# Ring weight slots 64 bytes longer, split weights placed 0 or 64 bytes into them by their role, operand pairs in one tile

## The chip, the cores and the metric

The kernel runs on one core of one Trainium2 chip. The metric is the device time of one execution in microseconds (us); smaller is better. Several executions are taken of a kernel, and their median is compared.

## The reference, cut to what matters

Two transformer layers work on 512 latent and 256 context tokens of 1024 features, all in float32. Layer 0 mixes the tokens by grouped attention (16 query heads, 4 key heads), layer 1 by a gated linear recurrence in two directions (HGRN2). Each is followed by a feed-forward block, and shifts, scales and gates are computed from a condition vector.

```python
for i in range(DEPTH):
    mod_l = (silu(c) @ ada_w[i] + ada_b[i])          # 6 shifts, scales and gates, likewise for ctx
    hn_l = modulate(rms_norm(h, norm_mix_w[i]), sh1_l, sc1_l)
    y_l, y_c = attention_mixer(...) if i % 2 == 0 else hgrn2_mixer(...)
    h = h + gt1_l * y_l
    h = h + gt2_l * swiglu(modulate(rms_norm(h, norm_ffn_w[i]), sh2_l, sc2_l), ffn_w_in[i], ffn_w_out[i])
    ...                                              # hc likewise in layer 0
return rms_norm(h, final_norm_w)
```

## The kernel before, in words

**Three products for one.** TensorE takes its operands as pairs: a float32 tile is split into a rounded high part and the rest (`split`, line 88: ScalarE casts the high part at line 90, VectorE or GpSimd subtracts at line 95). `mm3` (lines 116 to 120) then issues three matmuls into one accumulator: line 118 multiplies high by high, line 119 the high held part by the low streamed part, line 120 the low held part by the high streamed part. The operand that is loaded into the array with LDWEIGHTS, 128x128, is called held here, and the one that passes through it, 128 partitions by 256, 384 or 512 elements, streamed. The profile writes `out<-streamed,held`.

**Where operands lie.** Weights arrive by DMA in a ring of buffers: four slots `raw`, three `whi` and three `wlo`, each of 1024 floats per partition (4096 bytes), handed out in turn by the pool `ring` (`load_split`, line 99; `ring_tile`, line 1010). Normalized activations lie in pools of their own: `hnh`/`hnl` (attention input), `xb11`, `xb21`, `xb12`, `xb22`, `xw`, `xt1` to `xt4` (feed-forward operands, each with a high and a low tile), `gh`/`gl` (hidden units). Some pools begin with a tile named `shift` of 16 or 24 floats that nothing reads; it moves the pool's other tiles by 64 or 96 bytes.

**The stages, in order of time.** Attention: `kv` and `q` (activations held, weights streamed), `sc` (scores), softmax with its scaling on GpSimd (line 779), transposes `pt<-ident,pf` (line 789), `po`, then the projections `wo` and `wos`. Feed-forward 0, by a two-level scheme of seven products on half-size blocks (`x`, `y`, `z`, `w`; weights held, activations streamed at a width of 384) after some plain columns `ffi`; its output `ffo` has widths 256 and 512. HGRN: projections `hv`, `hg` (activations held, weights streamed, width 256), `hq`, `hz` (weights held, activations streamed, widths 512 and 256), the scan `lv` (line 1730), `hwo`. Feed-forward 1: as before, `ffi`, `x`, `y`, `z`, `w` at a width of 256, and `ffo` at 512 from `foh`/`fol`, whose slots are reused every second unit (`split_next`, line 1290).

**What sets the order.** A scheduler orders each engine's instructions by readiness and by when slots come free; two tiles that are parts of one allocation share their release. `residual` (line 760) adds a finished `ffo` to the stream `hT` on VectorE. `modc` holds the modulation columns (one tile per layer); four small fills of it are on GpSimd (line 263).

Of the kernel before, what the change touches and what calls it, by code (L numbers as in the profile page):

```python
# [16 lines left out]
P = 128  # L17
D = 1024
# [26 lines left out]
TAIL_BUDGET = (8, 1.6)  # L45
LEVELS = [1, 2, 4, 8, 16, 32, 64]
# [3 lines left out]
def kernel(  # L50
# [48 lines left out]
    def load_split(src, shape, name, eng=None, hi_eng=None):  # L99
        n = 1  # L100
        for s in shape[1:]:
            n *= s

        def get(kind, dt, bufs):
            t = ring.tile([P, 1024], dt, tag=kind, bufs=bufs, name=f"{kind}_{name}")
# [65 lines left out]
    csil = cst.tile([P, 2, KT], F32, name="csil")  # L171

# [30 lines left out]
    def ada_chunk(ch, pa, rows, load):  # L203
# [8 lines left out]
        ada_put(pa, rows(), modc[0][:, ch : ch + 1], ada_bias(0, ch, 1), 1, KT, pt)  # L212

    def ada_acc(layer, ch, nv, fp, wide):
# [38 lines left out]
        def folded():  # L253
            pc = bank(f"adc{layer}{ch}")
            mv = part[:, 0:nv].rearrange("p v (k j) -> p j k v", j=4)
            for j in range(4):
                PE.matmul(pc[32 * j : 32 * (j + 1), 0 : KT * nv], fold, mv[:, j], start=True, stop=True)
            DVE.tensor_tensor(
                modc[layer][:, ch, :, 0:nv], pc[:, 0 : KT * nv].rearrange("p (k v) -> p k v", v=nv),
                cols1[:, 32 + layer * 48 + ch * 8 :][:, 0:KT].unsqueeze(2).to_broadcast([P, KT, nv]), op=ALU.add,  # L260
            )
            if nv == 1:
                POOL.memset(modc[layer][:, ch, :, 1], 0.0)
# [45 lines left out]
    def modulate(es_pool, hs, rst, which, layer, hn_hi, hn_lo, spans):  # L309
        a_c = cst.tile([P, KT, 2], F32, name=f"a_{which}{layer}")  # L310
# [3 lines left out]
            a_c, modc[layer][:, csc], 1.0, nwv.unsqueeze(2).to_broadcast([P, KT, 2]),  # L314
# [27 lines left out]
    hn_hi, hn_lo = hn_tiles(hnp)  # L342
    qst = pool("qkvst", qes, side="right")
# [57 lines left out]
    a_c0 = cst.tile([P, KT, 2], F32, name="a_c0")  # L401
# [5 lines left out]
    def ada_group(gi, k0, n):  # L407
# [3 lines left out]
        for kk in range(0, KT, per):  # L411
# [28 lines left out]
    def ada_shared(ch, nsum):  # L440
# [113 lines left out]
    qT = [qt_tile(g) for g in range(KVH)]  # L554
    kTt = keep.tile([P, 2 * KVH, T], F32R, name="kT")
# [208 lines left out]
    ap_.tile([P, 16], F32, name="shift")  # L764
# [41 lines left out]
    def wo_gen(g, oh, ol):  # L806
        wo = [load_split(attn_w_o[0, k * P : (k + 1) * P, :], [P, D], f"wo{k}", POOL) for k in (2 * g, 2 * g + 1)]
# [27 lines left out]
    def third(h, t):  # L835
# [5 lines left out]
        if h % 2 == 1 and t == NT - 1:  # L841
# [30 lines left out]
    acc_n = pool("accn").tile([P, T], F32, name="acc_n")  # L872
# [76 lines left out]
    def ffn(layer, only_lat, pre, begin, tail=None):  # L949
# [7 lines left out]
        if layer:  # L957
            fp.tile([P, 16], F32, name="shift")

        def operand(m, slot=None):  # L960
# [6 lines left out]
            return [p_.tile([P, 4, H], F32R, tag=f"x{slot or m}{c}", name=f"x{m}{c}") for c in "hl"]  # L967
# [42 lines left out]
        def ring_tile():  # L1010
            return [ring.tile([P, 1024], F32R, tag=t, bufs=3, name=f"{t}_w") for t in ("whi", "wlo")]
# [975 lines left out]
```

## Time and profile before

| | us |
|---|---|
| median of three executions | 1793.43 |
| lowest and highest of them | 1792.02, 1795.57 |
| the profiled execution's own time | 1796.98 |
| its span, first to last instruction | 1795.1 |
| TensorE matmul busy | 1738.7 (97%) |
| TensorE weight loads busy, beside the matmuls | 1594.5 (89%) |
| VectorE busy | 1304.2 (73%) |
| ScalarE busy | 871.7 (49%) |
| GpSimd busy | 623.6 (35%) |

The profiled execution lies 3.55 us above the median, and 1.88 us of it lie outside the span. A matmul's listed duration reaches from its start to its modelled end and overlaps the next matmul; what a row of matmuls costs is the distance from start to start, which the timeline of TensorE shows.

### The profile page before, as it was taken

How to read it: one execution, taken by the hardware profiler on the slowest of the kernel's cores; microseconds unless marked ns; L12 is line 12 of the kernel's file. 1: busy time of each engine (PE TensorE's matmuls, PEld its weight loads, DVE VectorE, ACT ScalarE, POOL GpSimd, SP SyncE). 2: the span in 40 equal slices, each digit the busy share in tenths (PEclk: the TensorE clock that was granted, in tenths of full speed). 3: DMA queues.
4: the chain of work that ended last, by engine and by line, in shares of the span. 5: the costliest groups of instructions: out<-in, count | busy, mean ns of one | idle time of the engine just before them, and what ended most of it. 6: DMA issues, size and time to landing. Idle time of an engine off the chain costs nothing.

```text
span 1795.1 us, 30616 instructions
## 1 busy us (share of the span) xinstructions
PE 1738.7 (97%) x11717; PEld 1594.5 (89%) x11717; DVE 1304.2 (73%) x2281; ACT 871.7 (49%) x1777; POOL 623.6 (35%) x570
## 2 busy tenths in 40 slices
PE   8999999999999999999999999999999899999998
PEld 5788788988899989999998989898898898999996
DVE  4876688888888878887866565665747659886764
ACT  3454777776632524343345444343434445554545
POOL 1354355444112404131313343234425454433420
PEclk9999999999999999999999999999999899999999
DMA  8543410002034243445331122122211123333322
GB/s 310 192 130 119 152 36 25 24 1 77 24 106 124 69 131 94 150 133 159 100 118 46 60 71 64 54 83 84 77 53 46 58 60 115 101 111 105 100 61 84
DMA packets 213457, 166.42 MB, mean 93 GB/s; under 512 B 7952, under 2 KB 190400, under 8 KB 213312
## 3 DMA queue, kind: packets, MB, share of 16 engines
q1 hardware_dynamic: 213024, 163.43, 29.7%
q8 instruction: 92, 1.51, 0.3%
q10 hardware_dynamic: 288, 1.05, 0.1%
q14 instruction: 53, 0.43, 0.1%
HBM read 162.36 MB, written 2.10 MB: 92 GB/s over the span
## 4 chain that ended last, share of the span: by engine, by line
PE 78%; DVE 8%; ACT 5%; issue 3%; POOL 3%; DMA 1%; SPq 0%; POOLq 0%; DVEq 0%; ACTq 0%
PE ffo L118 5%; PE ffo L120 5%; PE ffo L119 5%; PE x L120 3%; PE x L119 3%; PE x L118 3%; PE lv L1730 3%; PE pt L789 3%; PE y L118 2%; PE y L119 2%; PE y L120 2%; PE hz L119 2%; PE hz L118 2%; PE hz L120 2%; PE sc L729 1%
## 5 line engine op out<-in xcount | busy, mean ns | idle before, releaser
L1737 POOL TENSOR_TENSOR KD<-KD,tot 128x384 f32<-128x384 f32 x96 | 102.5, 1091 | 79.9 <-ACT kc L1720 76.1
L779 POOL TENSOR_SCALAR pf<-pf,st 128x768 f32<-128x768 f32 (+1 forms) x96 | 73.6, 769 | 125.5 <-DVE st L778 89.3
L761 DVE SCALAR_TENSOR_TENSOR hT<-ffo,modc,hT 128x512 f32<-128x512 f32 (+1 forms) x122 | 78.4, 648 | 43.5 <-PE ffo L120 43.4
L120 PE MATMUL ffo<-gh,wlo_w 128*128 128x512 f32 (+1 forms) x304 | 102.4, 337 | 0.0
L119 PE MATMUL ffo<-gl,whi_w 128*128 128x512 f32 (+1 forms) x304 | 102.1, 336 | 0.0
L118 PE MATMUL ffo<-gh,whi_w 128*128 128x512 f32 (+1 forms) x304 | 101.8, 338 | 0.0
L242 DVE SCALAR_TENSOR_TENSOR adacc<-adw,csil,adacc 128x512 f32<-128x512 f32 x98 | 83.2, 859 | 8.7 <-DMA adw<-in_ada_w_dram 8.6
L95 DVE TENSOR_TENSOR ptl<-pt,pth 128x384 fp32r<-128x384 f32 (+1 forms) x160 | 79.8, 523 | 12.5 <-ACT pth L90 11.3
L90 ACT CAST pth<-pt 128x384 fp32r<-128x384 f32 (+1 forms) x160 | 69.9, 461 | 33.9 <-PE pt L789 22.1
L777 ACT ACTIVATE pf<-sc,st 128x768 f32<-128x768 f32 (+1 forms) x96 | 73.5, 765 | 18.9 <-DVE st L775 18.0
L1737 DVE TENSOR_TENSOR QD<-QD,tot 128x256 f32<-128x256 f32 x96 | 52.5, 587 | 40.6 <-PE lv L1730 40.4
L775 DVE TENSOR_REDUCE st<-sc 128x1 f32<-128x768 f32 (+1 forms) x96 | 74.0, 772 | 10.1 <-PE sc L730 8.7
L1720 ACT COPY kc<-KD 128x256 f32<-128x256 f32 x112 | 43.3, 413 | 75.2 <-PE lv L1730 44.8
L789 PE MATMUL pt<-ident,pf 128*128 128x128 f32 x448 | 72.2, 275 | 5.1 <-DVE ptl L95 3.8
L118 PE MATMUL ffo<-gh,foh 128*128 128x512 f32 (+1 forms) x186 | 71.3, 383 | 0.0
L120 PE MATMUL ffo<-gh,fol 128*128 128x512 f32 (+1 forms) x186 | 70.6, 380 | 0.2 <-DVE fol L95 0.2
L119 PE MATMUL ffo<-gl,foh 128*128 128x512 f32 (+1 forms) x186 | 70.7, 380 | 0.0
L1730 PE MATMUL lv<-QD,kc 128*128 128x128 f32 x448 | 63.8, 287 | 4.5 <-DVE QD L1737 2.3
L1796 POOL TENSOR_SCALAR oss<-oss 128x4 f32<-128x4 f32 (+1 forms) x9 | 4.7, 524 | 180.2 <-DVE oss L1795 180.1
L1730 PEld LDWEIGHTS lv<-QD,kc 128*128 128x128 f32 x448 | 59.1, 192 | 8.5 <-issue 4.3
L789 PEld LDWEIGHTS pt<-ident,pf 128*128 128x128 f32 x448 | 51.4, 140 | 13.8 <-issue 6.2
L120 PEld LDWEIGHTS ffo<-gh,wlo_w 128*128 128x128 f32 x304 | 57.3, 188 | 6.6
(1114 smaller groups left out, 6762.3 us busy)
## 6 DMA issues: line engine op xcount, KB each, us to landing
adw<-in_ada_w_dram SPq DMA_DIRECT2D x40, 512.0 KB, 4.6
adw<-in_ada_w_dram SPq DMA_DIRECT2D x80, 256.0 KB, 2.9
raw_hz<-in_hgrn_w_in_dram SPq DMA_DIRECT2D x14, 512.0 KB, 3.8
adr<-in_ada_w_dram SPq DMA_DIRECT2D x16, 256.0 KB, 5.9
adr<-in_ada_w_dram SPq DMA_DIRECT2D x8, 512.0 KB, 7.3
raw_wq<-in_attn_w_qkv_dram SPq DMA_DIRECT2D x8, 512.0 KB, 4.8
raw_wo<-in_attn_w_o_dram SPq DMA_DIRECT2D x8, 512.0 KB, 3.5
raw_hv<-in_hgrn_w_in_dram SPq DMA_DIRECT2D x8, 512.0 KB, 5.1
```

Of the source, the lines that this page charges most:

```text
L95: m = (eng or DVE).tensor_tensor(lo, src, hi.bitcast(F32), op=ALU.subtract)
L118: PE.matmul(ps, ahi, bhi, start=first, stop=False, **kw)
L119: PE.matmul(ps, ahi, blo, start=False, stop=False, **kw)
L120: PE.matmul(ps, alo, bhi, start=False, stop=last, **kw)
L242: pin(DVE.scalar_tensor_tensor(a, raw, cc, a, op0=ALU.mult, op1=ALU.add))
L761: DVE.scalar_tensor_tensor(hT[o][:, a:e], ps, mcol(layer, ch, o, v), hT[o][:, a:e], op0=ALU.mult, op1=ALU.add)
L775: DVE.tensor_reduce(st3[:, 0:1], ps[:, :nk], op=ALU.max, axis=AX.X, negate=True)
L777: ACT.activation(pf, ps[:, :nk], AF.Exp, bias=st3[:, 0:1], accum_out=st3[:, 1:2])
L779: POOL.tensor_scalar(pf, pf, st3[:, 2:3], 1.0, op0=ALU.mult, op1=ALU.mult)
L789: PE.transpose(pt[:, i * P : (i + 1) * P], pf[:, (i0 + i) * P : (i0 + i + 1) * P], ident)
L1730: PE.matmul(ps[:, cs], kc[:, cs], mv, start=True, stop=True)
L1737: eng.tensor_tensor(view, view, f, op=ALU.mult)
```

## The change

Per partition, a ring slot of `whi` and `wlo` gets 1040 floats in place of 1024. `ring_pair` hands out 1024 of them, beginning at float 0 or 16 of the slot; a table of which of the three slots lies where (`RING_BASE`) decides between the two so that a weight that is streamed begins at 0 modulo 128 bytes, and one that is held (`still=1`) at 64. High and low parts of a feed-forward operand, of a normalized HGRN operand and of an `fo` weight share one tile, again with an offset by role. The modulation columns of both layers share one tile `modc` of seven columns (layer 1's sixth uses the seventh), the scale tiles are renamed to one name `a_c`, and pads `shift`, `shift0` to `shift3` are added where others go.

```diff
+SHIFT = 16
+RING_BASE = {"whi": (1, 1, 0), "wlo": (0, 0, 1)}
...
+    def ring_pair(name, still):
+        got = []
+        for tag, bases in RING_BASE.items():
+            off = SHIFT if bases[pairs[0] % 3] != still else 0
+            t = ring.tile([P, 1024 + SHIFT], F32R, tag=tag, bufs=3, name=f"{tag}_{name}")
+            got.append(t[:, off : off + 1024])
+        pairs[0] += 1
+        return got
...
-        raw, hi, lo = get("raw", F32, 4), get("whi", F32R, 3), get("wlo", F32R, 3)
+        raw = view(ring.tile([P, 1024], F32, tag="raw", bufs=4, name=f"raw_{name}"))
+        hi, lo = map(view, ring_pair(name, still))
...
-    modc = [cst.tile([P, 6, KT, 2], F32, name=f"modc{l}") for l in range(2)]
+    modc = cst.tile([P, 7, KT, 2], F32, name="modc")
+
+    def mods_of(layer, chunk):
+        return modc[:, 6 if layer and chunk == 5 else chunk]
...
-                POOL.memset(modc[layer][:, ch, :, 1], 0.0)
+                POOL.memset(mods_of(layer, ch)[:, :, 1], 0.0)
...
-    ap_.tile([P, 16], F32, name="shift")
...
-        wo = [load_split(attn_w_o[0, k * P : (k + 1) * P, :], [P, D], f"wo{k}", POOL) for k in (2 * g, 2 * g + 1)]
+        wo = [load_split(attn_w_o[0, k * P : (k + 1) * P, :], [P, D], f"wo{k}", POOL, still=int(g == 0))
+              for k in (2 * g, 2 * g + 1)]
...
-        if layer:
-            fp.tile([P, 16], F32, name="shift")
+        def xpair(p_, tag, name, still):
+            if p_ is hnp:
+                return hn_pair(tag, name, still)
+            t = p_.tile([P, 8 * H + 32], F32R, tag=f"x{tag}", name=f"x{name}")
+            at = 16 * still
+            return [t[:, at : at + 4 * H], t[:, at + 4 * H : at + 8 * H]]
...
         def ring_tile():
-            return [ring.tile([P, 1024], F32R, tag=t, bufs=3, name=f"{t}_w") for t in ("whi", "wlo")]
+            return ring_pair("w", 1)
...
-                    tiles[ti] = [fp.tile([P, 640], F32R, tag=f"fo{c}", bufs=2, name=f"fo{c}") for c in "hl"]
+                    t = fp.tile([P, 1280 + 32], F32R, tag="fo", bufs=2, name="fo")
+                    tiles[ti] = [t[:, 16:656], t[:, 656:1296]]
                 elif ti not in tiles:
-                    tiles[ti] = [fp.tile([P, 3 * 512], F32R, tag=f"x{ti}{c}", name=f"fo{ti}{c}") for c in "hl"]
+                    tiles[ti] = xpair(fp, ti, f"fo{ti}", 1)
...
-    hnp.tile([P, 16], F32, name="shift")
+    hn_base = {"b11": 0, "b21": 1, "t4": 0, "b22": 1}
+
+    def hn_pair(tag, name, still):
+        t = hnp.tile([P, 8 * 384 + SHIFT], F32R, tag=f"x{tag}", name=f"x{name}")
+        at = SHIFT if hn_base[tag] != still else 0
+        return [t[:, at : at + 1536], t[:, at + 1536 : at + 3072]]
```

What the edits do to addresses can be read from the tile addresses of the two built programs. The table gives, for each group of matmuls, the first byte of the streamed and of the held operand modulo 128, before and after, and how many matmuls it holds. The last two rows are float32 matmuls, counted as the profile does, twice for each non-transpose.

| group (width) | matmuls | before: streamed, held | after |
|---|---|---|---|
| q (256) | 576 | 0, 96 | 0, 64 |
| hv, hg (256) | 960 | 0, 64 | 0, 64 |
| hz (256 and 512), hq (512) | 840 | 64, 0 | 64, 0 |
| x, y, z, w of feed-forward 1 (256) | 1512 | 64, 0 | 0, 64 |
| x, y, z, w of feed-forward 0 (384) | 1680 | 64, 0 | 0, 64 |
| ffo from ring weights (256; 512) | 456; 456 | 64, 0 | 0, 64 |
| ffo from foh, fol, fot (256; 512) | 132; 570 | 64, 64 | 0, 64 |
| ffi from ring weights (256) | 240 | 64, 0 | 0, 64 |
| ffi from w01, w11 (256) | 144 | 64, 64 | 0, 64 |
| hwo, wo (256; 512) | 240; 288 | 0, 0 | 0, 64 or 64, 0 |
| wos (384) | 96 | 0, 0 | 0, 64 |
| ffi of feed-forward 0 (384), a quarter each | 48; 48 | 64, 64 | 0, 64; 0, 0 |
| kv (512) | 144 | 0, 96 | 0, 64 |
| po (256) | 448 | 64, 0 | 0, 64 |
| sc (256; 512) | 192; 128 | 0, 0 | 0, 64 |
| transposes pt (128) | 448 | 0, 64 | 0, 0 |
| scan lv of line 1730 (128) | 448 | 96, 96 | 32, 32 |

The order of instructions on TensorE, ScalarE and SyncE's queue stays. Two engines have rows that move. On VectorE, near the end of feed-forward 1 (`residual` is line 761 before and 779 after; the split of an output weight is line 95 before and 97 after), before:

```order
2063 L761 SCALAR_TENSOR_TENSOR hT_1979<-ffo,modc_83,hT_1979 128x512
2064 L95 TENSOR_TENSOR fol<-raw_('fo', 4, 2)_18754,foh 128x640
2065 L95 TENSOR_TENSOR fol<-raw_('fo', 4, 3)_18760,foh 128x640
2066 L761 SCALAR_TENSOR_TENSOR hT_1980<-ffo,modc_83,hT_1980 128x512
2067 L279 TENSOR_TENSOR acc_n<-acc_n,sq_18944 128x512
```

and after:

```order
2063 L779 SCALAR_TENSOR_TENSOR hT_1981<-ffo,modc,hT_1981 128x512
2064 L779 SCALAR_TENSOR_TENSOR hT_1982<-ffo,modc,hT_1982 128x512
2065 L97 TENSOR_TENSOR fo<-raw_('fo', 4, 2)_18696,fo 128x640
2066 L97 TENSOR_TENSOR fo<-raw_('fo', 4, 3)_18701,fo 128x640
2067 L296 TENSOR_TENSOR acc_n<-acc_n,sq_18879 128x512
```

The second residual now stands ahead of the two splits. The same swap of one split and one residual occurs at the splits `('fo', 0, 2)` and `('fo', 0, 4)` at the start of feed-forward 1. On GpSimd the four fills of `modc` stand together at the program's start before:

```order
13 L165 TENSOR_TENSOR fold<-ident 128x32
14 L436 MEMSET pick 128x64
15 L263 MEMSET modc_83 128x8 x4
16 L167 TENSOR_TENSOR fold<-fold,ident 128x32
17 L438 MEMSET pick 128x1 x2
```

After, one stays there, one stands among the softmax scalings, and two at the start of feed-forward 0, of which this is the first (line 97 is the split's subtraction, 296 the sum of squares, 280 the fill):

```order
186 L296 TENSOR_TENSOR acc_n<-acc_n,sq_5473 128x384
187 L280 MEMSET modc 128x8
188 L97 TENSOR_TENSOR xb_5270<-x_5493,xb_5270 128x384
189 L311 TENSOR_TENSOR rc<-rc,mhalf 128x3
```

Three fills have moved to later rows. No other row has moved there, and no row was added or dropped on any engine.

Because the high and the low part of `fo` are now one tile, the ScalarE cast of a new high part waits for the last matmul that reads the slot's low part (line 120) and no longer for the one before it that reads the high part (line 119).

More of the change, by code (lines that the diff above doesn't have):

```diff
@@ L102, in load_split, with view @@
             n *= s
-        def get(kind, dt, bufs):
-            t = ring.tile([P, 1024], dt, tag=kind, bufs=bufs, name=f"{kind}_{name}")
+        def view(t):
             t = t[:, :n]
@@ L211, in ada_chunk @@
             yield
-        ada_put(pa, rows(), modc[0][:, ch : ch + 1], ada_bias(0, ch, 1), 1, KT, pt)
+        ada_put(pa, rows(), modc[:, ch : ch + 1], ada_bias(0, ch, 1), 1, KT, pt)
     def ada_acc(layer, ch, nv, fp, wide):
@@ L400 @@
     DVE.tensor_copy(cols1, pr[:, 0:P])
-    a_c0 = cst.tile([P, KT, 2], F32, name="a_c0")
+    a_c = cst.tile([P, KT, 2], F32, name="a_c")
     adv = ada_w[0].rearrange("(k p) (ch n) -> p k ch n", p=P, ch=6)
@@ L554 @@
     qT = [qt_tile(g) for g in range(KVH)]
+    keep.tile([P, SHIFT], F32, name="shift1")
     kTt = keep.tile([P, 2 * KVH, T], F32R, name="kT")
@@ L966, in operand @@
                 return [wide_op[0][:, i], wide_op[0][:, i + 1]]
-            return [p_.tile([P, 4, H], F32R, tag=f"x{slot or m}{c}", name=f"x{m}{c}") for c in "hl"]
+            if not layer and m == "t2":
+                return [p_.tile([P, 4, H], F32R, tag=f"x{m}{c}", name=f"x{m}{c}") for c in "hl"]
+            return [v_.rearrange("p (k n) -> p k n", k=4) for v_ in xpair(p_, slot or m, m, 0)]
         wide_op = []
         xops = {m: operand(m, slot) for m, slot in (("b11", None), ("b21", None), ("b12", "t4"), ("b22", None))}
-        a_c = cst.tile([P, KT, 2], F32, name=f"a_ffn{layer}")
         DVE.scalar_tensor_tensor(
-            a_c, modc[layer][:, 4], 1.0, cols1[:, 16 + layer * KT :][:, 0:KT].unsqueeze(2).to_broadcast([P, KT, 2]),
+            a_c, mods_of(layer, 4), 1.0, cols1[:, 16 + layer * KT :][:, 0:KT].unsqueeze(2).to_broadcast([P, KT, 2]),
             op0=ALU.add, op1=ALU.mult,
@@ L983, in gslot @@
         def gslot(i, dt, name):
-            p_ = late_pool[0] if not layer and i in (0, 1, 8, 9) else fp
-            return p_.tile([P, n], dt, tag=f"g{i}", name=name)
+            late = not layer and i in (0, 1, 8, 9)
+            t = (late_pool[0] if late else fp).tile([P, n], dt, tag=f"g{i}", name=name)
+            if late and i not in late_pool:
+                late_pool.append(i)
+                if len(late_pool) == 5:
+                    late_pool[0].tile([P, SHIFT], F32, name="shift3")
+            return t
         raws, loads, groups = {}, [], {}
@@ L1024, in plain_split @@
                 slot, p_ = {(0, 1): (3, fp), (1, 0): (1, fp), (1, 1): (2, fp if layer else hnp)}[j, i]
-                t = [p_.tile([P, 4 * H], F32R, tag=f"xt{slot}{c}", name=f"w{j}1{c}")[:, 0:1024] for c in "hl"]
+                if p_ is hnp:
+                    t = [p_.tile([P, 4 * H], F32R, tag=f"xt{slot}{c}", name=f"w{j}1{c}")[:, 0:1024] for c in "hl"]
+                else:
+                    t = [v_[:, 0:1024] for v_ in xpair(p_, f"t{slot}", f"w{j}1", 1)]
             pool_ = (j, i) == (0, 0) or j > 1 and i if layer else j == 0
@@ L1820, in wo_pair @@
     def wo_pair(pr_):
-        wo = [load_split(hgrn_w_o[0, k * P : (k + 1) * P, :], [P, D], f"hwo{k}") for k in (2 * pr_, 2 * pr_ + 1)]
+        wo = [load_split(hgrn_w_o[0, k * P : (k + 1) * P, :], [P, D], f"hwo{k}", still=1) for k in (2 * pr_, 2 * pr_ + 1)]
         if pr_ == GH // 2 - 2:
@@ L1838, in hgrn_wo_last @@
         for k in ks:
-            t = [ring.tile([P, 1024], F32R, tag=tag, bufs=3, name=f"{tag}_hwo{k}") for tag in ("whi", "wlo")]
+            t = ring_pair(f"hwo{k}", 1)
             split(t[0], t[1], hv.pop(("w", k)))
```

30 lines of the change are left out of this document (17 added, 13 removed).

## The prediction

> **What bounds the kernel now.** The page comes first: engines, the clock in 40 slices, and the chain that ended last.
>
> ```profile
> span 1795.1 us, 30616 instructions
> PE 1738.7 (97%) x11717; PEld 1594.5 (89%) x11717; DVE 1304.2 (73%) x2281; ACT 871.7 (49%) x1777; POOL 623.6 (35%) x570
> PEclk9999999999999999999999999999999899999999
> PE 78%; DVE 8%; ACT 5%; issue 3%; POOL 3%; DMA 1%; SPq 0%; POOLq 0%; DVEq 0%; ACTq 0%
> ```
>
> TensorE is busy 97% of the span, at a clock granted in full nearly throughout, and 78% of the chain is its own. So the time is the number of matmuls times the distance from one to the next. The change leaves the number and the order on TensorE alone. It can only pay through that distance, and the distance must then depend on addresses, for it alters nothing else there.
>
> The timeline of TensorE shows that the distance differs within one width. Here is the plain `ffi` stage of feed-forward 1 at width 256. Weights of `w11` (held at 64, streamed at 64) come first, then ring weights (held at 0) under the same line numbers.
>
> ```profile
> 1458.08 0.28 PE L118 MATMUL ffi<-xb22h,w11h 128*128 128x256 f32 x1
> ...
> 1458.44 0.28 PE L118 MATMUL ffi<-xw,whi_w 128*128 128x256 f32 x1
> ...
> 1459.46 0.28 PE L118 MATMUL ffi<-xw,whi_w 128*128 128x256 f32 x1
> ```
>
> Three matmuls take 0.36 us where both operands share their residue modulo 128, so 120 ns each; the nine after them take 1.02 us, 113.3 ns each. Next the first and last rows of four other runs at width 256: `hv` (15 steps, streamed 0, held 64), `x` and `z` of feed-forward 1 (19 steps, 64, 0), `q` (14 steps, 0, 96), `hwo` (15 steps, 0, 0).
>
> ```profile
> 998.82 0.28 PE L120 MATMUL hv<-whi_hv,hnb21l 128*128 128x256 f32 x1
> ...
> 1000.52 0.28 PE L120 MATMUL hv<-whi_hv,hnb22l 128*128 128x256 f32 x1
> ```
>
> ```profile
> 1599.73 0.28 PE L118 MATMUL x<-xw,whi_w 128*128 128x256 f32 x1
> ...
> 1601.96 0.28 PE L119 MATMUL z<-xw,whi_w 128*128 128x256 f32 x1
> ```
>
> ```profile
> 149.76 0.28 PE L118 MATMUL q<-whi_wq,hnh 128*128 128x256 f32 x1
> ...
> 151.40 0.28 PE L120 MATMUL q<-whi_wq,hnl 128*128 128x256 f32 x1
> ```
>
> ```profile
> 1419.78 0.28 PE L120 MATMUL hwo<-oth,wlo_hwo 128*128 128x256 f32 x1
> ...
> 1421.56 0.28 PE L120 MATMUL hwo<-oth,wlo_hwo 128*128 128x256 f32 x1
> ```
>
> That is 1.70/15 = 113.3 ns for `hv`, 2.23/19 = 117.4 for `x`, 1.64/14 = 117.1 for `q` and 1.78/15 = 118.7 for `hwo`. `hv` and `q` are the same code shape with other addresses. There are thus three paces: 113.3 (fast), about 117.3 (slow), 119 to 120 (same residue). The `ffi` run and `x` show that the first two are not told apart by addresses alone: both are 64 against 0.
>
> **The change, part by part.**
>
> *Width 256.* All these groups go to 0 against 64, as `hv` and `hg` have it, except `hz`, one pair of `wo` tiles and some small groups. How often such a group keeps the fast pace I read from means over whole groups, by the view that groups by line and shape:
>
> ```profile
> L119 PE MATMUL hv<-wlo_hv,hnb21h 128*128 128x256 f32 x48 | 13.3, 277 | 0.0
> L120 PE MATMUL x<-xw,wlo_w 128*128 128x256 f32 x72 | 20.1, 280 | 0.0
> L120 PE MATMUL ffi<-xb12h,wlo_w 128*128 128x256 f32 x20 | 5.5, 276 | 0.0
> ```
>
> The durations keep the distances' differences: 276 for a run that is all fast, 280 all slow, and `hv` at 277. It holds the fast pace for about three quarters of its matmuls. I take this share for every group that gets `hv`'s addresses. The sum, each count from the table of groups and the price as slow distance minus 113.3: `x`, `y`, `z`, `w` of feed-forward 1, 1512 x 4.1 ns = 6.2 us; `q`, 576 x 3.8 = 2.2; `ffo` of feed-forward 0, whose rows follow, 456 x (1.65 us/14 - 113.3 = 4.6) = 2.1; `hwo` and `wo`, 240 x 5.4 = 1.3; the 276 with equal residues, 276 x 6.7 = 1.8. Together 13.6, of which three quarters are **10.2 us** gained. `po` and `sc` wait too often in their rows for a price; they are taken at nothing, with 448 x 3.3 = 1.5 more as the other bound.
>
> ```profile
> 546.32 0.28 PE L118 MATMUL ffo<-gh,whi_w 128*128 128x256 f32 x1
> ...
> 547.97 0.28 PE L120 MATMUL ffo<-gh,wlo_w 128*128 128x256 f32 x1
> 548.09 0.40 PE L118 MATMUL ffo<-gh,whi_w 128*128 128x512 f32 x1
> ...
> 548.79 0.39 PE L118 MATMUL ffo<-gh,whi_w 128*128 128x512 f32 x1
> ```
>
> [...]
>
> *Widths 384 and 512.* First and last rows of a run of 11 steps of `foh` in feed-forward 1, then groups by line and shape:
>
> ```profile
> 1757.01 0.39 PE L118 MATMUL ffo<-gh,foh 128*128 128x512 f32 x1
> ...
> 1759.50 0.39 PE L120 MATMUL ffo<-gh,fol 128*128 128x512 f32 x1
> ```
>
> ```profile
> L120 PE MATMUL z<-xb21h,wlo_w 128*128 128x384 f32 x80 | 26.9, 336 | 0.0
> L120 PE MATMUL wos<-o,wlo_wo 128*128 128x384 f32 x32 | 10.8, 338 | 0.0
> L119 PE MATMUL hwo<-otl,whi_hwo 128*128 128x512 f32 x48 | 19.1, 398 | 0.0
> L120 PE MATMUL hz<-hnb11h,wlo_hz 128*128 128x512 f32 x28 | 11.0, 394 | 0.0
> ```
>
> No 384 and no 512 has 0 against 64 now. `wos` (0, 0) stands 2 ns above `z` (64, 0): with the 96 of `ffi` that share residues, 192 x 2 = 0.4 us gained. At 512, `hwo` at equal residues stands 4 ns above `hz`; waits may swell it, so I take half for the 288 of `hwo` and `wo` and the 144 of `kv`: 432 x 2 = 0.9 gained. The 1680 and 1026 others I take at nothing. Their bounds: the 384s could gain 336 against 336 - 3, as the 256s do (5.0 us), or lose the 2 ns of `wos` (3.4); `foh` at equal residues already runs 2.49 us/11 = 226.4 ns, below the 233.3 of `ffo` above (0.70/3), so it can lose 6.9 x 570 = 3.9 us and gain nothing, and the 456 can gain 3.1.
>
> *Transposes.* Line 789's pair moves from different to equal residues; `lv` has equal ones in before and after.
>
> ```profile
> L1730 PEld LDWEIGHTS lv<-QD,kc 128*128 128x128 f32 x448 | 59.1, 192 | 8.5 <-issue 4.3
> L789 PEld LDWEIGHTS pt<-ident,pf 128*128 128x128 f32 x448 | 51.4, 140 | 13.8 <-issue 6.2
> ```
>
> ```profile
> 302.67 0.49 PE L789 MATMUL pt<-ident,pf 128*128 128x128 f32 x3
> 1181.17 1.05 PE L1730 MATMUL lv<-QD,kc 128*128 128x128 f32 x8
> ```
>
> The weight load (the page's rows) would grow by 52 ns, hidden behind the matmul before (0 us) or in line (448 x 52 = 23). The lengths of unbroken runs (the timeline's rows) decide near 0: with one matmul at some 0.27, two steps of `pt` take 0.22 and seven of `lv` 0.78, 110 and 111.4 ns. **0.5 us** lost (448 x 1.4 = 0.6, rounded).
>
> *The tail.* The timelines of ScalarE, VectorE and TensorE around the last pair of units:
>
> ```profile
> 1759.74 0.73 ACT L90 CAST foh<-raw_('fo', 4, 2)_18754 128x640 fp32r<-128x640 f32 x1 [4.06 <-PE ffo L119]
> ```
>
> ```profile
> 1759.93 0.75 DVE L761 SCALAR_TENSOR_TENSOR hT<-ffo,modc,hT 128x512 f32<-128x512 f32 x1 [3.79 <-PE ffo L120]
> 1760.60 0.81 DVE L95 TENSOR_TENSOR fol<-raw_('fo', 4, 2)_18754,foh 128x640 fp32r<-128x640 f32 x1
> ```
>
> ```profile
> 1761.47 0.50 PE L120 MATMUL ffo<-gh,fol 128*128 128x512 f32 x1 [0.20 <-DVE fol L95]
> ```
>
> TensorE waits here for the split `fol`, which starts 0.67 us after the residual. With a second residual ahead of it the split starts another 0.67 later, and the matmul behind it too, on the chain: **0.7 us** lost. The cast's wait for line 120 rather than 119 costs one step of 0.23; it ends before the second residual does, so the 0.7 holds it. Behind it on ScalarE is queued the cast for unit ('fo', 4, 3), which TensorE needs one unit later, after fifteen matmuls of some 0.23 us, 3.4 in all. At the other two swaps and for the other casts the slot's next use is a unit or more ahead: nothing, or 0.67 apiece if that cover is gone.
>
> *GpSimd's fills.* One fill, by the view of its tile, and the row that one of them will stand ahead of:
>
> ```profile
> L263 POOL MEMSET modc<- x4: 105/106/107, 2.0 to 2.1; 128x8 f32 x4
> ...
> 438.39 1.01 POOL L95 TENSOR_TENSOR xb11l<-x,xb11h 128x384 fp32r<-128x384 f32 x1 [1.80 <-ACT xb11h L90]
> ```
>
> The fill, 0.11 us, goes ahead of this row and into its 1.80 us of idle time; what hides it is the wait for ScalarE. The merged `modc` and `a_c` and the pads issue nothing. All at nothing, or 0.3 us if the three fills were in line.
>
> Sum: -10.2 - 0.4 - 0.9 + 0.5 + 0.7 = **-10.3 us**. On the profiled execution, 1796.98 - 10.3 = 1786.7; on the median, 3.55 lower, 1793.43 - 10.3 = **1783.1 us**.
>
> **The rivals.**
>
> *Residues alone.* The slow pace is a state that a run falls into whatever its addresses, as `x` and `ffi` at one pair of residues suggest, and only equal residues are a cost by themselves. Then the gain is 144 x 6.7 (`ffi`, in a fast stage) = 1.0, 132 x 2.6 (120 to 117.4) = 0.3, 240 x 1.3 = 0.3, 0.4 and 0.9, in all 2.9 against 1.2 lost: -1.7, 1791.7 us; 1790.1 if `q`, which has `hv`'s form, takes its pace as well (2.2 x 3/4). For it: feed-forward 1 and `ffi`. Against: `q` and `hv`, alike but for addresses.
>
> *Streaming from 0 slows the wide ones* (the other side). The slowest 512 rows, `hwo` among them, stream from 0, the fastest, `foh`, from 64, and the change makes nearly all stream from 0. With the bounds above, `foh` loses 3.9 and the 384s 3.4; of the 256s only 1.0 + 0.3 + 0.3 is gained, and 1.2 lost elsewhere: +6.9, 1800.3 us. It decides from 1.8 ns on each of these 2250 matmuls (4.0 us, less the 0.4 that the rest nets). Against it: `hv` streams from 0 and is the fastest at its width.
>
> *Addresses do nothing*, and the paces come from something else in each stage. Then the tail alone remains: +0.7, 1794.1 us. [...] The triple at 1458.08 to 1458.44 speaks against it: 120 and 113.3 ns in one stage, where only the held weight's tile changes.
>
> **How the numbers follow.** Within 0.2%, 3.6 us, a change of this kernel cannot be told from none. The full sum has 0.45: it rests on `hv` as the one group that has the new addresses now. Residues alone 0.35, wide ones slower 0.13, nothing 0.07. Faster by over 3.6 us is the first case and a little of the second (0.08): 0.53. Slower is most of the third: 0.11. The rest, 0.36, is the same. The likeliest case's own range is 1778 (the 384s gain 5) to 1787 (half of 13.6 in place of three quarters). For 8 in 10 the range reaches from 1780 past residues alone and nothing, to 1795, leaving out the slower case and the first one's far end.
>
> **What would show it.** Right: in the profile after, `x`, `y`, `z`, `w` at width 256 near 277 in place of 280 and their starts 113 to 114 ns apart from 1500 on, `q` likewise, matmul-busy time lower by about 10 us, and the wait of `ffo` line 120 for the split grown from 0.20 to about 0.9. Residues alone: `x` stays at 280, only `hwo`, `wos` and the `ffi` of `w11` fall. Slower: starts of `foh` 233 ns apart rather than 226, `z` at width 384 at 338. Wrong in the step that carries most: a feed-forward 1 at 117.4 with `hv` still at 113.3.

## The result, and the profile after

| | before | after |
|---|---|---|
| median, us (12 executions of each) | 1793.78 | 1797.33 |
| lowest and highest, us | 1792.02, 1796.11 | 1794.52, 1800.4 |
| ratio to before, 95% interval | | 1.0019 [1.001, 1.0028] |
| profiled execution, us | 1796.98 | 1796.98 |

The change makes the kernel slower by 3.55 us (1.8 to 5.0 by the interval), where 10.3 us less were forecast; the time lies above the range given. One profiled execution differs from another by more than that: the two profiles have spans of 1795.1 and 1795.2 us, and a later profile of the unchanged kernel has 1789.0. TensorE's mean granted clock differs with them: 0.992 in the first profile of before, 0.994 in the later one. So spans are not compared here. What repeats is the distance from matmul to matmul: in two profiles of the unchanged kernel the means of the groups below agree within 0.3 ns.

The page of the kernel after, in the parts that were shown of before:

```profile
span 1795.2 us, 30613 instructions
PE 1739.7 (97%) x11717; PEld 1594.3 (89%) x11717; DVE 1302.9 (73%) x2281; ACT 871.3 (49%) x1777; POOL 625.2 (35%) x570
PEclk9999999999999999999999999999999899999999
PE 77%; DVE 9%; ACT 4%; issue 4%; POOL 3%; DMA 2%; SPq 0%; POOLq 0%; DVEq 0%; ACTq 0%
```

TensorE is the bound as before, with the same number of matmuls and the same clock in the 40 slices (mean granted 0.992 before, 0.993 after); its busy time, which should have fallen by about 10 us, stands at 1739.7 for 1738.7. Now the groups by line and shape that the prediction read (busy us, mean ns of one):

```profile
L132 PE MATMUL hv<-wlo_hv,xnb 128*128 128x256 f32 x144 | 40.3, 280 | 0.0
L133 PE MATMUL x<-xw,wlo_w 128*128 128x256 f32 x72 | 20.1, 279 | 0.0
L133 PE MATMUL w<-xt,wlo_w 128*128 128x256 f32 x72 | 20.0, 278 | 0.0
L133 PE MATMUL z<-xb,wlo_w 128*128 128x384 f32 x80 | 26.9, 336 | 0.0
```

`x` and `w` have come down only from 280 to 279 and 278, and `hv`, the model for all of them, has itself gone up from 277 to 280. The timeline of TensorE shows both kinds of run: here `hv` (21 steps), `z` running into `y` at the start of feed-forward 1 (23 steps) and `hq` at width 512 (7 steps), first and last row of each.

```profile
1001.20 0.40 PE L132 MATMUL hq<-xnb,whi_hq 128*128 128x512 f32 x1
...
1002.82 0.39 PE L133 MATMUL hq<-xnb,wlo_hq 128*128 128x512 f32 x1
...
1100.03 0.28 PE L133 MATMUL hv<-whi_hv,xnb 128*128 128x256 f32 x1
...
1102.51 0.28 PE L133 MATMUL hv<-whi_hv,xnb 128*128 128x256 f32 x1
...
1500.55 0.28 PE L131 MATMUL z<-xw,whi_w 128*128 128x256 f32 x1
...
1503.16 0.28 PE L133 MATMUL y<-xt,wlo_w 128*128 128x256 f32 x1
```

`hv` now runs at 2.48/21 = 118.1 ns where before stood at 113.3, `hq` at 1.62/7 = 231.4, while the stretch from `z` to `y` does run at 2.61/23 = 113.5. The same run of `hq` in the repeated profile of before takes 1.61/7 = 230.0 (the rows are rounded to 0.01 us, so seven steps resolve 1 to 2 ns; the means further down decide):

```profile
1000.87 0.39 PE L119 MATMUL hq<-hnt4l,whi_hq 128*128 128x512 f32 x1
...
1002.48 0.40 PE L120 MATMUL hq<-hnb22h,wlo_hq 128*128 128x512 f32 x1
```

The means over whole groups, from the starts in the timeline of TensorE, steps with a wait left out, in ns. The third and fourth columns are worked out from the tile addresses of the two built programs: the address of the operand that the next matmul holds less that of the one streamed now, modulo 256 bytes, here called the distance. Why it is shown comes with the experiments; that the next matmul's operand is meant, and not the present one's, is a choice here; at width 512 the trace of after bears it out, as shown there too.

| group (width) | matmuls | distance before | after | pace before | after |
|---|---|---|---|---|---|
| hv; hg (256) | 576; 384 | 64 | 64 and 192 | 114.2; 114.8 | 117.5; 117.1 |
| q (256) | 576 | 224 | 64 and 192 | 117.1 | 116.9 |
| x, y, z, w (256) | 1512 | 192; 64 in half of `y` | 64 and 192 | 117.5 to 117.8 | 115.1 to 116.3 |
| ffo (256) | 588 | 192, 64, 0, 128 | 64 and 192 | 117.8 | 116.6 |
| ffi (256) | 384 | 192, 0, 128 | 64 and 192 | 115.6 | 117.0 |
| x, y, z, w (384) | 1680 | 192 | 64 and 192 | 173.3 to 173.4 | 173.9 to 174.4 |
| ffo (512) | 1026 | 0, 192, 64, 128 | 64 and 192 | 230.0 | 231.5 |
| hq (512) | 168 | 192 | 64 and 192 | 229.4 | 231.9 |

A long run of width 384 shows the loss there, before (first two rows) and after, 335 steps of feed-forward 0:

```profile
678.86 0.34 PE L118 MATMUL x<-xb11h,whi_w 128*128 128x384 f32 x1
...
736.94 0.34 PE L120 MATMUL x<-xt3h,wlo_w 128*128 128x384 f32 x1
...
677.02 0.34 PE L131 MATMUL x<-xb,whi_w 128*128 128x384 f32 x1
...
735.33 0.34 PE L133 MATMUL x<-xt,wlo_w 128*128 128x384 f32 x1
```

That is 58.08/335 = 173.4 ns before and 58.31/335 = 174.1 after. And the eleven steps of `foh` at width 512 that the prediction read at 226.4 ns now take 2.53/11 = 230.0:

```profile
1756.41 0.39 PE L131 MATMUL ffo<-gh,fo 128*128 128x512 f32 x1
...
1758.94 0.40 PE L133 MATMUL ffo<-gh,fo 128*128 128x512 f32 x1
```

Last the tail, in the waits of TensorE after and in the timeline around the last pair of units:

```profile
PE ffo L133 <- DVE fo L97: 0.7, 1, 0.7
PE ffo L131 <- ACT fo L92: 0.2, 1, 0.2
```

```profile
1759.38 1.45 DVE L779 SCALAR_TENSOR_TENSOR hT<-ffo,modc,hT 128x512 f32<-128x512 f32 x2 [3.92 <-PE ffo L133]
...
1760.20 0.50 PE L131 MATMUL ffo<-gh,fo 128*128 128x512 f32 x1 [0.17 <-ACT fo L92]
...
1760.74 0.81 DVE L97 TENSOR_TENSOR fo<-raw_('fo', 4, 2)_18696,fo 128x640 fp32r<-128x640 f32 x1
...
1761.61 0.50 PE L133 MATMUL ffo<-gh,fo 128*128 128x512 f32 x1 [0.68 <-DVE fo L97]
```

The two residuals take 1.45 us in one stretch, the split starts behind them, and TensorE waits 0.17 for the cast and 0.68 for the split where it waited 0.20 in all: 0.65 us more.

### The profile page after: what moved, and what is told of

The parts are those of the page before. It is cut to its first block, busy times and chain, and to the rows that moved or that the text cites. A ratio compares the mean times of both kernels' runs of the same rounds, so it can differ in the third digit from the quotient of the medians.

```text
span 1795.2 us, 30613 instructions
## 1 busy us (share of the span) xinstructions
PE 1739.7 (97%) x11717; PEld 1594.3 (89%) x11717; DVE 1302.9 (73%) x2281; ACT 871.3 (49%) x1777; POOL 625.2 (35%) x570
## 4 chain that ended last, share of the span: by engine, by line
PE 77%; DVE 9%; ACT 4%; issue 4%; POOL 3%; DMA 2%; SPq 0%; POOLq 0%; DVEq 0%; ACTq 0%
PE ffo L133 5%; PE ffo L131 5%; PE ffo L132 5%; PE x L131 3%; PE x L132 3%; PE x L133 3%; PE pt L806 3%; PE lv L1771 2%; PE y L131 2%; PE y L132 2%; PE y L133 2%; PE hz L131 2%; PE hz L132 2%; PE hz L133 2%; PE sc L747 1%
## 5 line engine op out<-in xcount | busy, mean ns | idle before, releaser
L133 PE MATMUL ffo<-gh,fo 128*128 128x512 f32 (+1 forms) x186 | 71.1, 382 | 0.7 <-DVE fo L97 0.7
L131 PE MATMUL ffo<-gh,fo 128*128 128x512 f32 (+1 forms) x186 | 71.6, 385 | 0.2 <-ACT fo L92 0.2
L132 PE MATMUL ffo<-gl,fo 128*128 128x512 f32 (+1 forms) x186 | 70.8, 380 | 0.0
L131 PE MATMUL x<-xt,whi_w 128*128 128x256 f32 (+1 forms) x224 | 67.3, 300 | 0.0
L132 PE MATMUL x<-xt,whi_w 128*128 128x256 f32 (+1 forms) x224 | 67.2, 300 | 0.0
L133 PE MATMUL x<-xt,wlo_w 128*128 128x256 f32 (+1 forms) x224 | 67.0, 299 | 0.0
```

The costliest lines, as they stand in the source:

```text
L131: PE.matmul(ps, ahi, bhi, start=first, stop=False, **kw)
L132: PE.matmul(ps, ahi, blo, start=False, stop=False, **kw)
L133: PE.matmul(ps, alo, bhi, start=False, stop=last, **kw)
```

## The experiments

Two theories stood against each other. **Residues** is the prediction's: what counts is where a matmul's own two operands begin modulo 128 bytes. **Distance** came from comparing the two traces: the slot that grew to 4160 bytes keeps every residue modulo 128 but moves by 64 modulo 256 from slot to slot, so most groups have a part of their steps at one distance and the rest at another. The runs below are compared with the kernel before, taken beside them.

**The kernel before, unchanged, once more**, for the spread of paces.

> The kernel before, unchanged, for a second profile. Three theories of the loss of 3.5 us: (A) the distance from a streamed operand to the next matmul's held operand, modulo 256 bytes rather than 128, sets the pace by width, and the change mixes distances that had been uniform; (B) the paces are a state of one execution, not of the addresses; (C) the shared tiles of high and low parts and their later waits cost it. A and C: hv again near 114 ns from start to start, x of feed-forward 1 near 117.7, the same as in the first profile within 0.5 ns; time ratio 1.000. B: the stages' paces come out differently, hv perhaps at 117.

1794.23 against 1793.97 us, 1.0002 [0.9993, 1.001]. `hv` has 114.2 and `x` 117.8 ns again. In these two executions a group's pace is thus a property of the program, not of the execution.

**The shared tiles alone**, with all residues as before:

```diff
-                    tiles[ti] = [fp.tile([P, 640], F32R, tag=f"fo{c}", bufs=2, name=f"fo{c}") for c in "hl"]
+                    t = fp.tile([P, 1280], F32R, tag="fo", bufs=2, name="fo")
+                    tiles[ti] = [t[:, 0:640], t[:, 640:1280]]
...
```

The pairs of the feed-forward and HGRN operands share a tile in the same way.

> Before, with the high and low parts of the feed-forward operands, the normalized HGRN operands and the fo weights each in one tile, and every operand at the residue that it had. C: slower by 2.5 to 3.5 us, as the whole change. A and B: only the tail's 0.9 us (the split behind a second residual 0.7, a cast 0.2), ratio about 1.0005, and paces as in before.

1794.94 against 1793.97 us, 1.0002 [0.9993, 1.0011], and the paces of before within 0.3 ns, but for `hv` (115.4) and a few small groups. No address modulo 256 of `hv` differs from before, so 1 to 2 ns in one group can come from elsewhere. The groups by line and shape show the tail's new wait as after has it:

```profile
L118 PE MATMUL ffo<-gh,fo 128*128 128x512 f32 x166 | 65.4, 394 | 0.2 <-ACT fo L90 0.2
L119 PE MATMUL ffo<-gl,fo 128*128 128x512 f32 x166 | 65.0, 392 | 0.0
L120 PE MATMUL ffo<-gh,fo 128*128 128x512 f32 x166 | 65.0, 392 | 0.7 <-DVE fo L95 0.7
```

So the wait comes from the shared `fo` tile, not from any address; it is too small for the ratio.

**One distance for all of feed-forward 1.** The second kernel of this pair alone has the longer pad:

```diff
-            fp.tile([P, 16], F32, name="shift")
+            fp.tile([P, 48], F32, name="shift")
+
+        def t1_tile(c):
+            return fp.tile([P, 4 * H + 64], F32R, tag=f"xt1{c}", name=f"xt1{c}")[:, 32 : 32 + 4 * H]
...
```

Without the pad, all of `x`, `y`, `z`, `w` (where half of `y` was at 64) stand at distance 192:

> Before, with the operand xt1 of feed-forward 1 moved by 128 bytes, so that all of x, y, z, w there stream at one distance (192) from the next held weight; before, half of y had 64. Strong form of A (a mixture of distances keeps the pace slow): x, y, z, w stay at the 113.3 ns of the plain stage, up to 1512 x 4.3 = 6.5 us faster, ratio 0.9965. Weak form of A (each matmul is priced by its own distance alone): y of xt1 unchanged near 117.5, ratio 1.000. B: nothing that can be told.

1793.24 against 1793.97, 0.9995 [0.9986, 1.0004]; `x` and `y` at 117.5. Half a group at another distance was not what kept it slow; nor did the half of `y` at 64 in the kernel before have a pace of its own (117.7 at either distance). With the pad, all stand at 64, and the residues modulo 128 are those of before (64 streamed, 0 held):

> The same, with the pool's pad 48 floats instead of 16, so that all of x, y, z, w and the ring's ffi stream at distance 64, the one that hv has; fo keeps distance 0. Weak A: 117.2 to 115.1 ns on 1750 matmuls, 3.7 us faster, ratio 0.998. Strong A: 113.3 for most, 6 us faster. A rule by modulo 128 alone: the same as before, ratio 1.000.

1792.99 against 1793.97, 0.9995 [0.9987, 1.0004]. The paces move, though no residue modulo 128 did, which speaks against Residues: `x`, `y`, `z`, `w` 116.4 to 116.6. The mean is of two kinds of run. Two units in the timeline of TensorE, each with 47 steps from one `y` over `x` and `w` to the next `y`, and 11 or 14 of `ffo`:

```profile
1571.68 0.28 PE L118 MATMUL y<-xt1h,whi_w 128*128 128x256 f32 x1
...
1577.01 0.28 PE L120 MATMUL y<-xb22h,wlo_w 128*128 128x256 f32 x1
1577.13 0.39 PE L118 MATMUL ffo<-gh,foh 128*128 128x512 f32 x1
...
1579.69 0.40 PE L120 MATMUL ffo<-gh,fol 128*128 128x512 f32 x1
...
1646.51 0.28 PE L118 MATMUL y<-xt1h,whi_w 128*128 128x256 f32 x1
...
1652.05 0.28 PE L120 MATMUL y<-xb22h,wlo_w 128*128 128x256 f32 x1
1652.17 0.40 PE L118 MATMUL ffo<-gh,foh 128*128 128x512 f32 x1
...
1655.37 0.39 PE L120 MATMUL ffo<-gh,fol 128*128 128x512 f32 x1
```

From 1530 to 1598 us every unit has 113.4 ns at width 256 and `ffo` at 232.7; from 1601 to 1748 every one has 117.7 to 117.9, and `ffo` 228.6 or 232.1. So a pace is kept over many units, through the `ffo` in between, and it changes where the blocks of `ffo` change their length: fast with 12 matmuls in a block, slow with 9 before and 15 after. The distances inside these blocks change too and do not give the rule: all at 0 in the blocks of 9, half at 128 in those of 12, all at 0 in the first blocks of 15, half at 128 in the later ones. The plain `ffi`, at 64 now too, went the other way, from 115.6 to 118.6 (384 matmuls, 1.2 us lost of the 1.8 that 1512 x 1.2 ns gave), and the `ffo` of width 512 from `foh` and `fol` went from 229.2 to 230.4 at unchanged distances, 0.6 us more. By the paces nothing is left of the gain, and the ratio shows none.

**A table of the two addresses by themselves.** This kernel leaves the whole computation out: 24 matmuls in `mm3`'s order for each pair of addresses and each width.

```diff
+    for n in (256, 384, 512):
+        for h in (0, 64):
+            for s in range(0, 512, 64):
+                run(n, s, h)
+    for s in (64, 192, 320, 448):
+        for t in (0, 64, 128, 192):
+            run(256, s, 0, 8, f"then{t}", (256, t))
```

> A kernel of its own that leaves out the whole computation: 24 matmuls in the order of mm3 (held high, high, low; streamed high, low, high) for each width 256, 384, 512, each streamed residue 0 to 448 in steps of 64 (modulo 512) and held residue 0 or 64, a wait between the groups; then width 256 with twelve matmuls of another residue in the middle. The paces before are the same in a second execution (hv 114.2 and 114.2, x 117.7 and 117.8), so they are no chance of one execution. A (distance of the streamed operand to the next held one, modulo 256, by width): at 256 distance 64 has the shortest step, 192 some 2 ns more, 0 and 128 some 4; at 384 and 512 distance 192 is shorter than 64 by 1 to 2 ns, 128 longest; residues s and s+256 agree, and held 64 repeats held 0 shifted. Modulo 128 alone: distances 64 and 192 agree at every width. If the pace is kept by history, the third part of a group after twelve equal-residue matmuls stays slower than its first part.

With the held operand at 0, mean step in ns by the streamed operand's address (64 streamed is distance 192, and so on), the first steps of each group, before it settles, left out:

| width | distance 64 | 192 | 128 | 0 |
|---|---|---|---|---|
| 256 | 113.4 | 117.7 | 118.7 | 120.0 |
| 384 | 174.7 | 173.4 | 175.6 | 173.4 |
| 512 | 233.4 | 228.9 | 233.3 | 226.7 |

An address 256 higher gives the same figures within 0.8 ns. Two of the rows behind it, by line and shape: distance 64 and 192 at width 256, held at 0.

```profile
L93 PE MATMUL w256s192h0q<-X,W 128*128 128x256 f32 x8 | 2.2, 276 | 0.0
...
L93 PE MATMUL w256s64h0q<-X,W 128*128 128x256 f32 x8 | 2.2, 280 | 0.0
```

Both have the residues modulo 128 that `x` had before, 64 streamed and 0 held; their steps are 4.3 ns apart. And what is best at 256 is worst at 512. With the held operand at 64 the table is the same by distance within 1 ns, but for two entries at distance 64: width 384 has 176.7, and width 256 has 117.7 when streamed from 0, though 113.4 when streamed from 256.

The last three lines of the edit put twelve matmuls of another distance into the middle of a group at width 256. A group at 64 is back at 113.4 to 113.6 soon after them, so equal residues in its middle leave nothing behind. But twelve at distance 64 in the middle of a group at 192 do not reach 113.4:

```profile
268.30 0.28 PE L91 MATMUL w256s64h0then192q<-X,W 128*128 128x256 f32 x1
...
269.59 0.28 PE L93 MATMUL w256s64h0then192q<-X,W 128*128 128x256 f32 x1
```

These eleven steps take 1.29/11 = 117.3 ns. So already at one width a few steps at 64 keep the pace of the 192s around them.

**Mixed distances alone.** Ring slots 64 bytes longer as in the change, but placed so that every matmul keeps its residues modulo 128; no shared `x` or `fo` tiles.

```diff
+RING_OFF = {'whi': (0, 0, 16), 'wlo': (16, 16, 0)}
...
+            t = ring.tile([P, 1024 + 16], F32R, tag=tag, bufs=3, name=f"{tag}_{name}")
+            got.append(t[:, off : off + 1024])
```

> Before with ring slots 64 bytes longer and an offset of 0 or 64 bytes per slot such that every weight keeps its residue modulo 128, but the slots' residues modulo 256 are mixed, as they are after the change; nothing else moved, except that modc is one tile to make room. A: most of the change's loss comes back: hv and hg from 114.4 to 117, the 384s from 173.4 to 174.4, 3 to 5 us slower, ratio 1.0015 to 1.003. Modulo 128 alone, or shared tiles as the cause: ratio 1.000, paces as before.

1795.94 against 1793.89 us, 1.0012 [1.0003, 1.0021]: 2.05 of the change's 3.55 us, where 3 to 5 were expected. Its paces in these groups are near those of after: `hv` 117.4, `hg` 116.5, `x`, `y`, `z`, `w` 114.8 to 116.4 at width 256 and 174.1 to 174.7 at 384, `hq` 232.0. The rows of `hv` and `hq` by line and shape (`hv` had 277):

```profile
L132 PE MATMUL hv<-wlo_hv,hnb21h 128*128 128x256 f32 x48 | 13.5, 281 | 0.0
...
L133 PE MATMUL hq<-hnb21h,wlo_hq 128*128 128x512 f32 x14 | 5.5, 394 | 0.0
```

No residue modulo 128 differs from before. This settles it against Residues: the mixing of distances by the longer slot is enough for the slower paces of `hv`, `hg`, `hq` and the 384s.

In the kernel after itself the steps of a mixed group can be sorted by distance, from the starts in the timeline and the addresses of the built program. Mean step in ns:

| group (width) | at distance 64 | at 192 |
|---|---|---|
| x, y, z, w (384) | 175.0 | 173.5 |
| hq (512) | 233.6 | 230.1 |
| ffo (512) | 232.3 | 230.3 |
| hv (256) | 116.7 | 118.2 |
| q (256) | 116.1 | 118.2 |
| x, y, z, w (256) | 115.9 | 116.3 |

At 384 and 512 each step goes by its own distance, within 1.5 ns of the table by itself. At 256 the steps at 64 stay 2.5 ns or more above 113.4: beside steps at 192 they lose most of their advantage. Over all groups of width 512 together, a step that is followed by a held operand at distance 192 takes 230.0 ns (183 steps) where its own held operand is at 64, and 230.5 (735) where it is at 192; followed by one at 64, 232.3 and 232.4. So there the next matmul's operand counts and not the present one's. At width 256 no such order shows.

**The attention pad alone**, 32 bytes ahead of the normalized inputs; `q` and `kv` go from distance 224 to 192.

```diff
+    hnp.tile([P, 8], F32, name="shift0")
```

> Before with the change's 32-byte pad behind the attention inputs alone: q and kv from distance 224 to 192 and nothing else. A, weak: kv from 233.1 to near 230, 0.4 us; q within 1 ns of its 117.0, 0 to 0.6 us either way; ratio 0.9995 to 1.0003. The forecast's price of q (fast pace by its residue modulo 128): 1.6 us faster, ratio 0.999, q near 114.

1795.65 against 1793.89, 1.001 [1.0001, 1.0019]. The paces came near the table: `q` 117.8 (117.7 there), `kv` 229.6 (228.9 there). They nearly cancel: 576 x 0.7 ns lost, 144 x 3.5 gained. The 1.76 us (0.2 to 3.4 by the interval) are not explained by them, and stay open.

**Two blocks in turn**, because the pace in feed-forward 1 was carried. This kernel too leaves the whole computation out: 12 matmuls of width 256 and 9 of width 512, four times over, for each pair of distances, that of the 256s first.

```diff
+    for dx in (64, 192, 128, 0):
+        for df in (0, 64, 128, 192):
+            run(dx, df)
```

> A kernel of its own that leaves out the whole computation: four times in turn 12 matmuls of width 256 at distance dx and 9 of width 512 at distance df, as the last feed-forward has them, for dx and df each of 0, 64, 128, 192. In the kernels, x at one distance of 64 ran at 113.3 ns in some stretches and at 117.8 in others, the latter behind 512s that had settled at 226.7. If the pace is carried over from block to block: x at distance 64 behind 512s at distance 0 settles at 117.8, and behind 512s at another distance at 113.3 to 114. If each matmul is priced by its own distance alone: x at distance 64 is at 113.4 behind every 512, at 192 at 117.7, and the 512s at 226.7 (0), 228.9 (192), 232 to 233 (64, 128), as measured alone.

The 256s at distance 64 do not keep their 113.4. In the timeline of TensorE, a block of 11 steps with the 512s at 0, then one with the 512s at 64:

```profile
36.34 0.28 PE L84 MATMUL x64f0q<-X,W 128*128 128x256 f32 x1
...
37.64 0.28 PE L86 MATMUL x64f0q<-X,W 128*128 128x256 f32 x1
...
46.77 0.28 PE L84 MATMUL x64f64q<-X,W 128*128 128x256 f32 x1
...
48.02 0.28 PE L86 MATMUL x64f64q<-X,W 128*128 128x256 f32 x1
```

1.30/11 = 118.2 and 1.25/11 = 113.6 ns, to within 1 ns by the rounding of the rows, with the same addresses in the block itself. At (64, 64) two of the four blocks have 113.6, at (64, 0), (64, 128) and (64, 192) none has, and at (192, 128) one has it. So the table's paces held throughout only in unbroken groups; behind blocks of another kind the pace went with those blocks as well, 118.2 and 113.6 ns above. Distance as first stated, a matter of one group alone, falls.

**One distance for `q`**: the pad at 160 bytes, on the kernel before, with the one `modc` of the change, which frees room. `q` has the residues that the change gives it (0 streamed, 64 held), at distance 64 throughout.

```diff
+    hnp.tile([P, 40], F32, name="shift0")
```

> Before, with modc as one tile and a pad of 160 bytes behind the attention inputs, so that q (and kv) stream at distance 64 from the next held operand instead of 224; nothing else moves. A: q from 117.0 towards the 113.4 that width 256 has alone at distance 64, 1 to 2 us faster, ratio 0.9990 to 0.9995; kv stays near 233. If the pace is carried over from the 512s and waits around it: q stays at 117 to 118, ratio 0.9997 to 1.0005.

1792.3 against 1794.18, 0.9991 [0.9981, 1.0], so the time alone is at the edge of showing a gain. `q` has 114.7 ns, where the change, with the same residues but both distances, has 116.9, and the kernel with the 32-byte pad, with these residues at distance 192 throughout, 117.8. That is one group with one pair of residues modulo 128 and three arrangements modulo 256. First and last of 39 steps in the timeline of TensorE:

```profile
148.38 0.28 PE L120 MATMUL q<-whi_wq,hnl 128*128 128x256 f32 x1
...
152.80 0.28 PE L120 MATMUL q<-whi_wq,hnl 128*128 128x256 f32 x1
```

4.42/39 = 113.3 ns: what the prediction expected of `q`, and what the change gave it in parts only.

**Both of the uniform arrangements**, feed-forward 1 and `q` at 64:

> That, and x, y, z, w of the last feed-forward at distance 64 with fo at distance 0, both as before otherwise. A: 1 us from the feed-forward (measured 116.6 on x) and 1 to 2 us from q, 2 to 3 us faster than before, ratio 0.9983 to 0.999; faster than before and after if so.

1791.6 against 1794.18 us, 0.9983 [0.9974, 0.9992]: faster than before by 2.6 us. `q` has 114.5 ns, `x`, `y`, `z`, `w` 116.4 to 116.5, `ffi` 118.6. By the paces `q` gives 1.5 us of it and feed-forward 1 nothing on balance; where the rest comes from is not shown.

**The output weights at 64 as well**, on feed-forward 1 at 64:

```diff
-                    tiles[ti] = [fp.tile([P, 640], F32R, tag=f"fo{c}", bufs=2, name=f"fo{c}") for c in "hl"]
+                    tiles[ti] = [fp.tile([P, 704], F32R, tag=f"fo{c}", bufs=2, name=f"fo{c}")[:, 16:656] for c in "hl"]
```

> x, y, z, w of the last feed-forward and its fo weights all at distance 64. By the table of blocks x alternates between 113.4 and 117.9 from block to block and the 512s of fo run at 232 to 233.7 instead of 226.7 to 230: 3 ns less on 1512 and 3 ns more on 498, 3 us faster than before in the feed-forward, less 1 us for its plain stage, ratio 0.999. If each matmul's own distance decides: x at 113.4 all through, 5 us faster, ratio 0.997.

1793.08 against 1794.18, 0.9993 [0.9983, 1.0004]. `x`, `y`, `z`, `w` come down to 115.6 to 115.8, and `ffo` from these weights goes up from 229.2 to 232.0: 1512 x 2.0 = 3.0 us gained, 498 x 2.8 = 1.4 and `ffi`'s 1.2 lost. Neither this kernel nor the one with `fo` at 0 gives the 256s and the 512s their best pace together.

## Why the prediction was wrong

The terms of its sum, and what the paces of the two profiles make of them (count times difference, all groups of a width together). Which steps are left out as waits moves the measured entry for width 256 between -0.8 and -1.2:

| term | forecast, us | measured, us |
|---|---|---|
| width 256 | -10.2 | -1.2 |
| width 384 | -0.4 | +0.8 |
| width 512 | -0.9 | +2.0 |
| transposes | +0.5 | 0 |
| tail | +0.7 | +0.7 |
| sum | -10.3 | +2.3 (the medians: +3.55, 1.8 to 5.0) |

**The step that failed** stands in the part on width 256: "It holds the fast pace for about three quarters of its matmuls. I take this share for every group that gets `hv`'s addresses." The groups got `hv`'s addresses modulo 128 only. `hv` had one distance, 64, throughout; after the change `hv` and the others have 64 and 192 in turn, because a slot of 4160 bytes is no multiple of 256, and a table that repairs this modulo 128 does not repair it modulo 256. `x`, `y`, `z` and `w` gained 2.6 us where three quarters of 6.2 were expected, `q` 0.1 where three quarters of 2.2 were, and `hv` and `hg`, at no term in the sum since their residues stayed, lost 576 x 3.3 + 384 x 2.3 = 2.8 us. The mixing kernel, with no residue modulo 128 changed, shows the same paces, and `q` at one distance shows that there the pace was to be had. For `x`, `y`, `z` and `w` this is not shown: at one distance of 64, with the residues of before, they ran at 116.4 to 116.6, no faster than mixed, so for them `hv`'s share fails even at `hv`'s distance; there the pace carried over from block to block, 113.4 ns in every unit for 68 us and then 117.7 to 117.9 for 147. The prediction had the warning in its own rows: `ffi` at 113.3 and `x` at 117.4 "are not told apart by addresses alone"; their distance is the same too, 192. Two smaller readings were wrong. In the triple at 1458.08 not "only the held weight's tile changes": the streamed tile changes as well, from `xb22h` to `xw`. And of the 240 `hwo` and `wo`, 96 stream from 64 and hold 0 after the change, by the addresses of the built program, so 0.4 us of the 10.2 had no ground.

**The wide groups, taken at nothing**, are the second step that failed. 1680 matmuls of width 384 lost 0.74 ns on average, 1.2 us, and 1026 of `ffo` at 512 lost 1.5 ns each, 1.5 us. The bounds had allowed for it (3.4 and 3.9 us), and the rival in which the wide ones go slower had the sign. Its mechanism, streaming from 0, is not what the runs show: in the table by itself 384 and 512 streamed from 0 against 0 are among the fastest (173.4 and 226.7 ns), and the mixing kernel slows the 384s from 173.3 or 173.4 to 174.1 or more and `hq` from 229.4 to 232.0 with streamed residues unchanged. Its point of 1.8 ns on each of 2250 was not reached, and its +6.9 us was too much because the 384s lost 0.74 ns of the 2 that it took, and the 570 `ffo` from `foh` and the like 1.7 of the 6.9.

**What held.** TensorE was the bound (busy 97% of the span before and after) and, but for the tail, the distances between matmuls are what moved. That addresses do nothing, the last of the rivals, is out by `q` and by the table of addresses. Groups with equal residues gained: `wos` went from 176.1 to 173.3 ns and `hwo` at width 256 from 118.7 to 115.1, with 2 ns and 5.4 ns forecast; at 512 `kv`, which had no equal ones, gained 1.2, and `wo` and `hwo` nothing. By the table of addresses equal residues are two cases: distance 128 is slow at every width (118.7, 175.6 and 233.3 ns), distance 0 only at 256 (120.0, for 173.4 and 226.7 at the others). The tail cost 0.65 us against 0.7, by the second residual ahead of the split, and the shared tile alone reproduced it. GpSimd's moved fills cost nothing that any wait shows, and two of the kernels with the merged `modc` were no slower than before. The transposes' 0.5 us, from equal residues, did not come: `pt`'s weight loads stayed at 140 ns.

**What stays open.** About 1.2 us of the 3.55 are in no pace and in no wait that I found, within the interval. Part of them may be the clock: over 82 executions of the unchanged kernel in the later batches a granted clock lower by 0.001 goes with about 1.2 us more, and the executions of after have 0.9924 on average, those 0.9932, so about 1 us by this estimate. Whether the change lowers the clock or chance did, no run shows. Why the pace in feed-forward 1 goes with the length of the `ffo` blocks, why `ffi` runs against the table, and where the pad of 32 bytes loses 1.76 us, no run here settles.

## What to carry to other kernels

Where matmuls stand back to back, compare their starts, not their durations (0.28 us listed here, 113 to 120 ns from start to start), and note both operands' addresses modulo 256, from slot to slot, before a pad or a longer slot is judged; keep buffers of a ring at a multiple of 256 bytes, so that one group has one distance (the longer slots alone took `hv` from 114.2 to 117.4 ns). A group may be given another's pace in a forecast only if the whole address pattern agrees, and not one residue of it: `q` with one pair of residues modulo 128 had 114.7, 116.9 and 117.8 ns. A measurement by itself of such a pace need not hold between blocks of another width (113.4 ns alone, 118.2 behind 512s at distance 0); alternate the blocks as the kernel does.

## What the runs showed of the hardware that was not expected

At one width and one clock (0.993 in the table's run), the settled step of an unbroken run depends on two addresses: 113.4 to 120.0 ns at width 256, 226.7 to 233.4 at 512, with the best distance at 64 for the one and at 0 for the other; one pair at distance 64, streamed from 0 and held at 64, has 117.7 all the same. The prediction went by residues modulo 128: with 64 streamed and 0 held by that count, the step in this table was 117.7 ns from address 64 and 113.4 from 192. With the held operand at 0 or at 64 the steps agree by distance within 1 ns but for two entries, so in this run the two addresses acted together; why, it does not show. A pace, once taken, can also last: 113.4 ns for 68 us and then 117.7 to 117.9 for 147 us in feed-forward 1, with all its `x`, `y`, `z`, `w` at distance 64.
